# Gated delta rule in 64-chunks: a full inverse per chunk, multiplied into values and keys ahead of the chain over the chunks

## The chip, the core and the metric

The kernel runs on one core of a Trainium2 chip. A core has a matrix engine (TensorE, PE in the profile; PEld is its weight load), a vector engine (DVE), a scalar engine (ACT), a small general engine (POOL) and a queue processor that mostly issues DMA transfers (SP). Each runs its own list of instructions in order and waits on semaphores for the others. The metric is the device time of one execution in microseconds (us), the median over runs; lower is better.

## What is computed

The program is a chain of network blocks. Only the first one is touched: a hybrid block that sums a gated delta rule (8 heads of 64, both directions over 256 positions, chunks of 64) and a dilated-window attention. After it come a feed-forward layer, two mixers and a mixture of experts. The part of the reference that the change reorders:

```python
def gated_delta_rule_chunked(q, k, v, g, beta):
    ...
    kb = k * beta[..., None]
    a_low = jnp.where(strict, jnp.einsum('nhcid,nhcjd->nhcij', kb, k) * decay, 0.0)
    tmat = lax.linalg.triangular_solve(eye + a_low, eye, lower=True, unit_diagonal=True)
    u = jnp.einsum('nhcij,nhcjv->nhciv', tmat, v * beta[..., None])
    w = jnp.einsum('nhcij,nhcjk->nhcik', tmat, kb * jnp.exp(g)[..., None])
    ...
    def step(state, inp):
        u_i, w_i, qk_i, qd_i, kd_i, gl_i = inp
        v_new = u_i - jnp.einsum('nhck,nhkv->nhcv', w_i, state)
        o_i = jnp.einsum('nhck,nhkv->nhcv', qd_i, state) + jnp.einsum('nhij,nhjv->nhiv', qk_i, v_new)
        state = state * jnp.exp(gl_i)[..., None, None] + jnp.einsum('nhck,nhcv->nhkv', kd_i, v_new)
        return state, o_i
```

## The kernel before

Every large product is a gemm in three passes (lines 403, 404, 405: high part by high part, low by high, high by low), whose weights come by DMA in halves of 512 KB (`wr`) and are split by ACT and DVE (line 376) into `wh` and `wl`. These gemms use PSUM tiles `g`. The delta rule uses PSUM tiles `m` (three of them), the attention tiles `a` (two).

`delta()` (line 627) runs in the phase `mix1` beside gemms and attention. For each 128-row half t of the sequence and each direction d it makes `AQ[t, d]`: per head the triangular factor and the masked q-k product of two chunks of 64. The 32x32 diagonal blocks of the factor go through DRAM to one row per block, are inverted on DVE by a loop of 31 steps (lines 737 and 738), stored (line 739), and loaded back (line 747; for d = 1 turned on DVE, line 750) as `DT`. Beside that `kd` (k by decay) and `bv` (v by beta) are made on POOL (lines 762, 763), and k and q with their decays on DVE (line 766), turned by transposes on PE (line 770) and copied by ACT (line 771) into `kqd[t, d]`.

`delta_chain()` (line 782) then walks four chunks per direction, the two directions in turn. A step s has: p1 = (k with decay) times the state (line 797) and its subtraction on DVE (798), the solve with two inverted 32-blocks, that is a product (802) and copy on ACT (803), a product with the off-diagonal block (807) and subtraction on DVE (809), a product (813) and copy on ACT (814); then the new contribution to the state `pS` (820), the output `po` of q times state (824) and of the masked product (827), the decay of the state and the sum on DVE (837, 838; in step 0 a copy, 834), and the copy or sum of the output (841, 843). All of these are fp32 matrix products on tiles of 32x32, 64x64 or 128x64 of the PE array; one of them shows as two PE instructions in the trace.

Nothing in the block waits for the chain before `delta_out()`, which comes after the attention. The order in which each engine gets its instructions isn't written out: a scheduler with its own cost estimates merges delta rule, attention and gemms.

Of the kernel before, what the change touches and what calls it, by code (L numbers as in the profile page):

```python
# [17 lines left out]
AF = mybir.ActivationFunctionType  # L18
OP = mybir.AluOpType
# [30 lines left out]
P2 = (2, 1)  # L50
P3 = (2, 4)
P4 = (0, 1)
MIX1 = {"m": 3, "a": 2}, dict(s4=7, s2=13, s1=2, at3=5, ap=6, aq=4, on=2, dT=4)
FFN = {"m": 4, "n": 1}, dict(s4=5, s2=15, xr=4, xh=5, xl=5)
MIX2 = {"m": 3, "h": 2}, dict(s4=5, hx=2, m4=2, m2=6, h2=5, ti=4, tc=4, y=3, tg=4, hs=2, mix=2, od=2, s1=7)
MOE = {"m": 4, "g2": 1}, dict(s4=5, s2=8, xr=14, xh=4, xl=4)
# [209 lines left out]
class Prog:  # L266
# [360 lines left out]
    def delta(self):  # L627
        nc, mm = self.nc, self.nc.tensor.matmul

        y, m, e, l = (self.t("ty", [128, 2, 16]) for _ in range(4))  # L630
# [10 lines left out]
        be = self.t("dbe", [128, 2, 16])  # L641
# [16 lines left out]
        dec = self.t("ddec", [128, 8, 4])  # L658
# [13 lines left out]
        AQ = {}  # L672
# [64 lines left out]
            nc.vector.tensor_tensor(pv, av(U, 32 * i + m, [[0, m], [1, n]]), av(Y, i, [[32, m], [0, n]]), OP.mult)  # L737
            nc.vector.tensor_tensor(yv, yv, pv, OP.subtract)
        nc.sync.dma_start(Yd, Y)
        DT = {}  # L740
        for t in range(2):
            for d in range(2):
                dt_ = self.t("dT", [128, 8, 32], bufs=4) if d == 0 else self.t("s1", [128, 8, 32])
                for r in range(4):
                    src = bass.AP(tensor=Yd.tensor, offset=Yd.offset + (d * 64 + t * 4 + r) * 1024,
                                  ap=[[32, 32], [8 * 1024, 8], [1, 32]])
                    nc.sync.dma_start(dt_[32 * r:32 * r + 32], src)
                if d == 1:
                    o = self.t("dT", [128, 8, 32], bufs=4)
                    nc.vector.transpose(o, dt_)  # L750
                    dt_ = o
                DT[t, d] = dt_

        kd, bv, kqd = {}, {}, {}
        for d in range(2):
            for t in range(2):
                kqd[t, d] = self.t("s4" if d else "x", [128, 4, 2, 128])
                bc = lambda s: s[:, :, None].to_broadcast([128, 8, 64])
                hv = lambda x: x.rearrange("p (h e) -> p h e", h=8)
                q, k, v = (hv(self.qkv[a, t]) for a in range(3))  # L760
                kd[t, d], bv[t, d] = (self.t("s2", [128, 8, 64]) for _ in range(2))
                nc.gpsimd.tensor_tensor(kd[t, d], k, bc(ek[:, d, t]), OP.mult)
                nc.gpsimd.tensor_tensor(bv[t, d], v, bc(be[:, t, 8 * d:8 * d + 8]), OP.mult)
                for j, (src, sc) in enumerate(((k, bE[:, d, t]), (q, eG[:, d, t]))):
                    tmp = self.t("s2", [128, 8, 64])
                    nc.vector.tensor_tensor(tmp, src, bc(sc), OP.mult)
                    tf = tmp.rearrange("p h e -> p (h e)")
                    pt = self.p("m", [128, 4, 128])
                    for b in range(4):
                        nc.tensor.transpose(pt[:, b], tf[:, b * 128:b * 128 + 128], self.ident)  # L770
                    nc.scalar.activation(kqd[t, d][:, :, j], pt, AF.Copy)

        St = []
        for d in range(2):
# [1 line left out]
            nc.gpsimd.memset(s_, 0.0)  # L776
            St.append(s_)
        self.od = [self.t("s2", [128, 512]) for _ in range(2)]
        chains = [self.delta_chain(d, AQ, DT, bv, kd, kqd, St[d], dec) for d in range(2)]
        for _ in zip(*chains):  # L780
            pass
    def delta_chain(self, d, AQ, DT, bv, kd, kqd, St, dec):

        nc, mm = self.nc, self.nc.tensor.matmul
        for s in range(4):
            c = s if d == 0 else 3 - s
            t, a = c // 2, c % 2
            p0 = 64 * a
            q0, q1 = (p0, p0 + 32) if d == 0 else (p0 + 32, p0)
            b1 = 1 if d == 0 else 0  # L790
            P, Q0, Q1 = slice(p0, p0 + 64), slice(q0, q0 + 32), slice(q1, q1 + 32)
            cs = slice(a * 64, a * 64 + 64)
            v = u = bv[t, d]
            if s:
                p1 = self.p("m", [128, 4, 128])
                for b in range(4):
                    mm(p1[P, b], kqd[t, d][:, b, 0, cs], St[:, b], start=True, stop=True)
                nc.vector.tensor_tensor(u[P], u[P], p1[P].rearrange("p b (q e) -> p (b q) e", q=2), OP.subtract)
            yield
            p2 = self.p("m", [128, 8, 64])  # L800
            for h in range(8):
                mm(p2[Q0, h], DT[t, d][Q0, h], u[Q0, h], start=True, stop=True, tile_position=(q0, q0))
            nc.scalar.activation(v[Q0], p2[Q0], AF.Copy)
            yield
            p3 = self.p("m", [128, 8, 64])
            for h in range(8):
                mm(p3[Q1, h], AQ[t, d][Q0, h, 0, 32 * b1:32 * b1 + 32], v[Q0, h], start=True, stop=True,
                   tile_position=(q0, q1))
            nc.vector.tensor_tensor(u[Q1], u[Q1], p3[Q1], OP.subtract)
            yield  # L810
            p4 = self.p("m", [128, 8, 64])
            for h in range(8):
                mm(p4[Q1, h], DT[t, d][Q1, h], u[Q1, h], start=True, stop=True, tile_position=(q1, q1))
            nc.scalar.activation(v[Q1], p4[Q1], AF.Copy)
            yield
            if s < 3:
                pS = self.p("m", [128, 4, 64])
                for h in range(8):
                    L = slice(64 * (h % 2), 64 * (h % 2) + 64)
                    mm(pS[L, h // 2], kd[t, d][P, h], v[P, h], start=True, stop=True)  # L820
            po = self.p("m", [128, 4, 128])
            for b in range(4):
                if s:
                    mm(po[P, b], kqd[t, d][:, b, 1, cs], St[:, b], start=True, stop=False)
                for q in range(2):
                    h = 2 * b + q
                    mm(po[P, b, 64 * q:64 * q + 64], AQ[t, d][P, h, 1], v[P, h], start=(s == 0),
                       stop=(s == 0 or q == 1))
            if s < 3:
                for par in range(2):  # L830
                    L = slice(64 * par, 64 * par + 64)
                    sv = St[L, :, par]
                    if s == 0:
                        nc.vector.tensor_copy(sv, pS[L])
                    else:
                        dc = dec[L, (a * 2 + t) * 2 + d]
                        nc.vector.tensor_tensor(sv, sv, dc[:, :, None].to_broadcast([64, 4, 64]), OP.mult)
                        nc.vector.tensor_tensor(sv, sv, pS[L], OP.add)
            of = po[P].rearrange("p b n -> p (b n)")
            if s < 2:  # L840
                nc.scalar.activation(self.od[t][P], of, AF.Copy)
            else:
                nc.vector.tensor_tensor(self.od[t][P], self.od[t][P], of, OP.add)
            yield
# [1001 lines left out]
```

## Time and profile before

| | before |
|---|---|
| median of 3 runs (lowest to highest) | 2248.69 us (2246.05 to 2254.61) |
| profiled execution: its time | 2250.07 us |
| profiled execution: span | 2248.1 us |
| PE busy | 2185.7 us, 97% of the span |
| DVE busy | 1807.0 us, 80% |
| ACT busy | 1386.9 us, 62% |
| POOL busy | 38.7 us, 2% |

The delta rule's work lies between about 65 and 266 us of the span. An "idle before" is the time an engine stood still ahead of a group, with the engine and line that ended it. PEclk is the granted clock of PE as a share of 2.4 GHz: 1.00 is 2.4 GHz, 0.50 is 1.2 GHz, and a value between is a stretch with both. In the timeline the second number is the time from a group's start to its modelled end; matmuls overlap, so what a group takes of the engine is read from its start to the next group's start.

### The profile page before, as it was taken

Reading aid. Unit: us, or ns where it says so; the run is one execution under the profiler, and the core shown is the slowest. Engines: PE = TensorE matmul, PEld = TensorE weight load, DVE = VectorE, ACT = ScalarE, POOL = GpSimd, SP = SyncE. Lnnn points to the kernel's source line nnn. Section 1 sums busy time; section 2 is a strip of 40 time slices with the busy share of each in tenths; the row PEclk is TensorE's granted clock in tenths of the full one; section 3 lists DMA queues with packets and bytes.
Section 4 is the critical chain, followed back from the end, with each engine's and each line's share of the span. In section 5 each row is a group of like instructions: output and inputs, shape, how many; then the busy total and the mean of one; then the engine's idle time right before and its main releaser. Section 6 shows DMA issues by size and latency. Waiting matters only on the chain. (4 is left out here: it accounts for less than half of the span.)

```text
span 2248.1 us, 33817 instructions
## 1 busy us (share of the span) xinstructions
PE 2185.7 (97%) x12426; PEld 1862.6 (83%) x12426; DVE 1807.0 (80%) x2618; ACT 1386.9 (62%) x1854; POOL 38.7 (2%) x72
## 2 busy tenths in 40 slices
PE   7999999999999999999899999999999999999998
PEld 7787898999798878899787888788888888888886
DVE  6894367899868876878778876789899998989897
ACT  4553355554456565544258555588778888877885
POOL 0120000000000000000000000000000000000000
PEclk9999799999999999999999999999999999999999
DMA  6442254889364446888853445899999999999993
GB/s 200 123 145 73 66 154 147 327 293 317 117 206 144 131 145 206 302 289 301 292 187 118 147 150 174 309 346 357 341 369 348 346 363 337 357 343 367 349 352 137
DMA packets 164149, 549.41 MB, mean 244 GB/s; under 512 B 26632, under 2 KB 29320, under 8 KB 163976
## 3 DMA queue, kind: packets, MB, share of 16 engines
q1 hardware_dynamic: 163976, 547.18, 69.6%
q8 instruction: 99, 1.62, 0.3%
q14 instruction: 74, 0.61, 0.1%
HBM read 544.95 MB, written 2.11 MB: 243 GB/s over the span
## 5 line engine op out<-in xcount | busy, mean ns | idle before, releaser
L376 ACT ACTIVATE wh<-wr 128x1024 fp32r<-128x1024 f32 (+1 forms) x343 | 351.6, 1028 | 307.8 <-PE g L405 156.5
L376 DVE TENSOR_TENSOR wl<-wr,wh 128x1024 fp32r<-128x1024 f32 (+1 forms) x343 | 406.1, 1189 | 142.5 <-ACT wh L376 138.6
L376 DVE TENSOR_TENSOR xl<-xr,xh 128x1024 fp32r<-128x1024 f32 x282 | 338.1, 1221 | 26.2 <-ACT xh L376 18.2
L376 ACT ACTIVATE xh<-xr 128x1024 fp32r<-128x1024 f32 x282 | 295.8, 1061 | 73.7 <-PE g L405 29.4
L403 PE MATMUL g<-wh,xTH 128*128 128x512 f32 (+2 forms) x744 | 283.0, 382 | 5.4 <-ACT xTH L471 4.8
L404 PE MATMUL g<-wl,xTH 128*128 128x512 f32 (+2 forms) x744 | 281.2, 378 | 2.4 <-DVE wl L376 2.4
L405 PE MATMUL g<-wh,xTL 128*128 128x512 f32 (+2 forms) x744 | 281.9, 379 | 0.3 <-DVE xTL L472 0.3
L376 DVE TENSOR_TENSOR wl<-xr,wh 128x1024 fp32r<-128x1024 f32 x194 | 232.9, 1221 | 20.6 <-ACT wh L376 15.5
L376 ACT ACTIVATE wh<-xr 128x1024 fp32r<-128x1024 f32 x194 | 203.8, 1061 | 53.5 <-PE g L405 25.0
L403 PEld LDWEIGHTS g<-wh,xTH 128*128 128x128 f32 x744 | 143.1, 193 | 26.3 <-ACT xTH L471 5.6
L404 PEld LDWEIGHTS g<-wl,xTH 128*128 128x128 f32 x744 | 143.2, 192 | 24.0 <-DVE wl L376 3.9
L405 PEld LDWEIGHTS g<-wh,xTL 128*128 128x128 f32 x744 | 143.0, 192 | 22.1 <-issue 2.4
L403 PE MATMUL g<-xh,s 128*128 128x512 f32 x400 | 158.2, 396 | 0.0
L405 PE MATMUL g<-xh,s 128*128 128x512 f32 x400 | 156.4, 391 | 0.0
L404 PE MATMUL g<-xl,s 128*128 128x512 f32 x400 | 156.4, 391 | 0.0
L403 PE MATMUL g<-xTH,wh 128*128 128x256 f32 x528 | 151.3, 287 | 0.5 <-ACT wh L376 0.5
L404 PE MATMUL g<-xTL,wh 128*128 128x256 f32 x528 | 151.0, 286 | 0.1
L405 PE MATMUL g<-xTH,wl 128*128 128x256 f32 x528 | 150.4, 285 | 0.1
L376 ACT ACTIVATE xh<-wr 128x1024 fp32r<-128x1024 f32 x113 | 118.0, 1059 | 48.3 <-PE m L405 12.8
L376 DVE TENSOR_TENSOR xl<-wr,xh 128x1024 fp32r<-128x1024 f32 x113 | 135.8, 1220 | 11.9 <-ACT xh L376 10.1
L1130 DVE SCALAR_TENSOR_TENSOR macc<-rawm,cond,macc 128x1024 f32<-128x1024 f32 x84 | 107.6, 1281 | 34.4 <-DMA rawm<-in_wm_dram 33.8
L403 PE MATMUL g<-wh,s 128*128 128x512 f32 x320 | 126.8, 396 | 0.4 <-ACT s L471 0.4
(536 smaller groups left out, 4870.7 us busy)
## 6 DMA issues: line engine op xcount, KB each, us to landing
xr<-in_we_dram SPq DMA_DIRECT2D x412, 512.0 KB, 6.4
wr<-in_wb_dram SPq DMA_DIRECT2D x210, 512.0 KB, 4.8
wr<-in_we_dram SPq DMA_DIRECT2D x116, 512.0 KB, 6.1
rawm<-in_wm_dram SPq DMA_DIRECT2D x96, 512.0 KB, 5.6
wr<-in_wa_dram SPq DMA_DIRECT2D x82, 512.0 KB, 4.7
wr<-in_wt_dram SPq DMA_DIRECT2D x48, 384.0 KB, 3.1
xr<-in_wa_dram SPq DMA_DIRECT2D x32, 512.0 KB, 6.4
xr<-in_wb_dram SPq DMA_DIRECT2D x32, 512.0 KB, 8.4
```

The source lines that it names most:

```text
L376: self.behind((nc.scalar.activation(h, r, AF.Copy), nc.vector.tensor_tensor(l, r, h.bitcast(F), OP.subtract)))
L403: mm(ps, lh, rh, start=first, stop=False)
L404: mm(ps, lh, rl, start=False, stop=False)
L405: mm(ps, ll, rh, start=False, stop=last)
L1130: i = nc.vector.scalar_tensor_tensor(acc, raw, ck, acc, OP.mult, OP.add)
```

## The change

A new function `inverses()` builds, for each t and d, the whole (transposed) inverse of the 64-blocks in a tile `TT[t, d]`: the inverted 32-blocks are copied by ACT (new line 804) onto the diagonal of a zeroed tile, and the off-diagonal block is two 32x32 products, py (new line 816) and px (822), with a sign change on DVE between them (819) and a copy by ACT behind (824). From it come, outside of the chain, W (766, copied by ACT in 767 into `kqd[t, d][:, :, 0]`) and U (772, copied in 773). Only q is still transposed on PE (755). The product of v with beta moves from POOL to DVE (758). A step of the chain has left: W times state (837) with its subtraction on DVE (838), q times state into `po` (843; now all four ahead, in the same accumulation group), the decay of the state (848), `pS` (853) and its addition (860), and the masked product (864). `s4` gets an eighth buffer.

```diff
--- before.py
+++ after.py
@@ -50,7 +50,7 @@
 P2 = (2, 1)
 P3 = (2, 4)
 P4 = (0, 1)
-MIX1 = {"m": 3, "a": 2}, dict(s4=7, s2=13, s1=2, at3=5, ap=6, aq=4, on=2, dT=4)
+MIX1 = {"m": 3, "a": 2}, dict(s4=8, s2=13, s1=2, at3=5, ap=6, aq=4, on=2, dT=4)
 FFN = {"m": 4, "n": 1}, dict(s4=5, s2=15, xr=4, xh=5, xl=5)
 MIX2 = {"m": 3, "h": 2}, dict(s4=5, hx=2, m4=2, m2=6, h2=5, ti=4, tc=4, y=3, tg=4, hs=2, mix=2, od=2, s1=7)
 MOE = {"m": 4, "g2": 1}, dict(s4=5, s2=8, xr=14, xh=4, xl=4)
@@ -737,38 +737,40 @@
             nc.vector.tensor_tensor(pv, av(U, 32 * i + m, [[0, m], [1, n]]), av(Y, i, [[32, m], [0, n]]), OP.mult)
             nc.vector.tensor_tensor(yv, yv, pv, OP.subtract)
         nc.sync.dma_start(Yd, Y)
-        DT = {}
-        for t in range(2):
+        TT = self.inverses(Yd, AQ)
+
+        kd, U, kqd = {}, {}, {}
+        for t in range(2):
+            bc = lambda s: s[:, :, None].to_broadcast([128, 8, 64])
+            hv = lambda x: x.rearrange("p (h e) -> p h e", h=8)
+            q, k, v = (hv(self.qkv[a, t]) for a in range(3))
             for d in range(2):
...
                 kqd[t, d] = self.t("s4" if d else "x", [128, 4, 2, 128])
...
+                tq, tk = self.t("s2", [128, 8, 64]), self.t("s2", [128, 8, 64])
+                kd[t, d], U[t, d] = (self.t("s2", [128, 8, 64]) for _ in range(2))
+                nc.vector.tensor_tensor(tq, q, bc(eG[:, d, t]), OP.mult)
+                tf = tq.rearrange("p h e -> p (h e)")
+                pt = self.p("m", [128, 4, 128])
+                for b in range(4):
+                    nc.tensor.transpose(pt[:, b], tf[:, b * 128:b * 128 + 128], self.ident)
+                nc.scalar.activation(kqd[t, d][:, :, 1], pt, AF.Copy)
+
+                nc.vector.tensor_tensor(U[t, d], v, bc(be[:, t, 8 * d:8 * d + 8]), OP.mult)
+                nc.vector.tensor_tensor(tk, k, bc(bE[:, d, t]), OP.mult)
                 nc.gpsimd.tensor_tensor(kd[t, d], k, bc(ek[:, d, t]), OP.mult)
...
+                for a in range(2):
+                    P = slice(64 * a, 64 * a + 64)
+                    pw = self.p("m", [128, 4, 64])
+                    for h in range(8):
+                        L = slice(64 * (h % 2), 64 * (h % 2) + 64)
+                        mm(pw[L, h // 2], tk[P, h], TT[t, d][P, h], start=True, stop=True)
+                    nc.scalar.activation(kqd[t, d][:, :, 0, P], pw, AF.Copy)
+                pu = self.p("m", [128, 8, 64])
+                for a in range(2):
+                    P = slice(64 * a, 64 * a + 64)
+                    for h in range(8):
+                        mm(pu[P, h], TT[t, d][P, h], U[t, d][P, h], start=True, stop=True)
+                nc.scalar.activation(U[t, d], pu, AF.Copy)
 
         St = []
         for d in range(2):
@@ -776,66 +778,91 @@
             nc.gpsimd.memset(s_, 0.0)
             St.append(s_)
         self.od = [self.t("s2", [128, 512]) for _ in range(2)]
-        chains = [self.delta_chain(d, AQ, DT, bv, kd, kqd, St[d], dec) for d in range(2)]
+        chains = [self.delta_chain(d, AQ, U, kd, kqd, St[d], dec) for d in range(2)]
         for _ in zip(*chains):
             pass
-    def delta_chain(self, d, AQ, DT, bv, kd, kqd, St, dec):
+    def inverses(self, Yd, AQ):
+
+        nc, mm = self.nc, self.nc.tensor.matmul
+        TT, TP = {}, {}
+        for t in range(2):
+            TP[t] = self.t("s4", [128, 2, 8, 64])
+            nc.gpsimd.memset(TP[t], 0.0)
+        for t in range(2):
+            for d in range(2):
+                T = TT[t, d] = TP[t][:, d]
+
+                raw, turned = (self.t("dT", [128, 8, 32], bufs=4) for _ in range(2))
+                for r in range(4):
+                    src = bass.AP(tensor=Yd.tensor, offset=Yd.offset + (d * 64 + t * 4 + r) * 1024,
+                                  ap=[[32, 32], [8 * 1024, 8], [1, 32]])
+                    nc.sync.dma_start(raw[32 * r:32 * r + 32], src)
+                nc.vector.transpose(turned, raw)
+                across, plain = (raw, turned) if d == 0 else (turned, raw)
+                for r in range(4):
+                    R4 = slice(32 * r, 32 * r + 32)
+                    nc.scalar.activation(T[R4, :, 32 * (r % 2):32 * (r % 2) + 32], across[R4], AF.Copy)
+
+                py, px = self.p("m", [128, 8, 32]), self.p("m", [128, 8, 32])
+                y = self.t("s1", [128, 8, 32])
+                b1 = 1 - d
+                blocks = []
+                for a in range(2):
+                    p0 = 64 * a
+                    q0, q1 = (p0, p0 + 32) if d == 0 else (p0 + 32, p0)
+                    blocks.append((q0, q1, slice(q0, q0 + 32), slice(q1, q1 + 32)))
+                for q0, q1, Q0, Q1 in blocks:
+                    for h in range(8):
+                        mm(py[Q1, h], AQ[t, d][Q0, h, 0, 32 * b1:32 * b1 + 32], plain[Q0, h], start=True, stop=True,
+                           tile_position=(q0, q1))
+                for q0, q1, Q0, Q1 in blocks:
+                    nc.vector.tensor_scalar(y[Q1], py[Q1], -1.0, None, OP.mult)
+                for q0, q1, Q0, Q1 in blocks:
+                    for h in range(8):
+                        mm(px[Q0, h], y[Q1, h], across[Q1, h], start=True, stop=True, tile_position=(q1, q0))
+                for q0, q1, Q0, Q1 in blocks:
+                    nc.scalar.activation(T[Q0, :, 32 * b1:32 * b1 + 32], px[Q0], AF.Copy)
+        return TT
+    def delta_chain(self, d, AQ, U, kd, kqd, St, dec):
 
         nc, mm = self.nc, self.nc.tensor.matmul
         for s in range(4):
             c = s if d == 0 else 3 - s
             t, a = c // 2, c % 2
...
+            P = slice(64 * a, 64 * a + 64)
+            v = U[t, d]
             if s:
                 p1 = self.p("m", [128, 4, 128])
                 for b in range(4):
-                    mm(p1[P, b], kqd[t, d][:, b, 0, cs], St[:, b], start=True, stop=True)
-                nc.vector.tensor_tensor(u[P], u[P], p1[P].rearrange("p b (q e) -> p (b q) e", q=2), OP.subtract)
+                    mm(p1[P, b], kqd[t, d][:, b, 0, P], St[:, b], start=True, stop=True)
+                nc.vector.tensor_tensor(v[P], v[P], p1[P].rearrange("p b (q e) -> p (b q) e", q=2), OP.subtract)
             yield
...
+            po = self.p("m", [128, 4, 128])
+            if s:
+                for b in range(4):
+                    mm(po[P, b], kqd[t, d][:, b, 1, P], St[:, b], start=(b == 0), stop=False)
+                if s < 3:
+                    for par in range(2):
+                        L = slice(64 * par, 64 * par + 64)
+                        sv, dc = St[L, :, par], dec[L, (a * 2 + t) * 2 + d]
+                        nc.vector.tensor_tensor(sv, sv, dc[:, :, None].to_broadcast([64, 4, 64]), OP.mult)
             if s < 3:
                 pS = self.p("m", [128, 4, 64])
                 for h in range(8):
                     L = slice(64 * (h % 2), 64 * (h % 2) + 64)
                     mm(pS[L, h // 2], kd[t, d][P, h], v[P, h], start=True, stop=True)
...
                 for par in range(2):
                     L = slice(64 * par, 64 * par + 64)
                     sv = St[L, :, par]
                     if s == 0:
                         nc.vector.tensor_copy(sv, pS[L])
                     else:
-                        dc = dec[L, (a * 2 + t) * 2 + d]
-                        nc.vector.tensor_tensor(sv, sv, dc[:, :, None].to_broadcast([64, 4, 64]), OP.mult)
                         nc.vector.tensor_tensor(sv, sv, pS[L], OP.add)
+            for b in range(4):
+                for q in range(2):
+                    h = 2 * b + q
+                    mm(po[P, b, 64 * q:64 * q + 64], AQ[t, d][P, h, 1], v[P, h], start=(s == 0),
+                       stop=(s == 0 or h == 7))
             of = po[P].rearrange("p b n -> p (b n)")
             if s < 2:
                 nc.scalar.activation(self.od[t][P], of, AF.Copy)
```

The order of PE in the middle of the delta rule. Before, in step 1 and 2 of the chain (`m` are the delta rule's PSUM tiles, `g` the gemms', `wh` and `wl` split weights, `x` and `s4` tiles at the right of 797 are `kqd`):

```order
L797 MATMUL m_242_1328<-s2_216_1094,x_195_1031 64x128 x4
L405 MATMUL g_498_2530<-wh_492_2519,xTL_4_69 128x512
L403 MATMUL g_498_2530<-wh_492_2519,xTH_3_68 128x512
L404 MATMUL g_498_2530<-wl_493_2520,xTH_3_68 128x512
L797 MATMUL m_243_1334<-s2_217_1096,s4_202_1052 64x128 x4
L405 MATMUL g_498_2530<-wh_492_2519,xTL_4_69 128x512
L403 MATMUL g_497_2529<-wh_495_2525,xTH_3_68 128x512
L802 MATMUL m_244_1340<-s2_197_1033,dT_185_998 32x64 x8
L802 MATMUL m_245_1350<-s2_204_1054,dT_184_996 32x64 x8
L404 MATMUL g_497_2529<-wl_496_2526,xTH_3_68 128x512
L405 MATMUL g_497_2529<-wh_495_2525,xTL_4_69 128x512
```

After, at the place where W and U are made, between the last gemms beside the inverses and the chain (`s4_182` and `s4_183` are the inverses, `s2_...` at the right of 766 the scaled k):

```order
L755 MATMUL m_218_1249<-ident_5_72,s2_214_1244 128x128 x4
L766 MATMUL m_219_1258<-s4_182_986,s2_215_1245 64x64 x8
L766 MATMUL m_220_1268<-s4_182_986,s2_215_1245 64x64 x8
L772 MATMUL m_221_1278<-s2_217_1247,s4_182_986 64x64 x16
L755 MATMUL m_227_1302<-ident_5_72,s2_223_1297 128x128 x4
L766 MATMUL m_228_1311<-s4_183_988,s2_224_1298 64x64 x8
L766 MATMUL m_229_1321<-s4_183_988,s2_224_1298 64x64 x8
L772 MATMUL m_230_1331<-s2_226_1300,s4_183_988 64x64 x16
L755 MATMUL m_236_1355<-ident_5_72,s2_232_1350 128x128 x4
L766 MATMUL m_237_1364<-s4_183_988,s2_233_1351 64x64 x8
L766 MATMUL m_238_1374<-s4_183_988,s2_233_1351 64x64 x8
L772 MATMUL m_239_1384<-s2_235_1353,s4_183_988 64x64 x16
```

Before, gemm instructions stand between the small products of a step; after, 12 groups of transposes, W and U follow each other with none between.

DVE at the first attention block, before (`aq` are the attention's q and k that PE turns next, `dbE` and `deG` decays):

```order
L719 STREAM_TRANSPOSE s2_177_909<-s2_178_910 128x512
L766 TENSOR_TENSOR s2_191_1015<-s2_75_471,dbE_139_757 128x512
L766 TENSOR_TENSOR s2_193_1023<-s2_51_313,deG_137_755 128x512
L556 TENSOR_TENSOR aq_282_1634<-aq_282_1634,ty_321_1808 128x384
L766 TENSOR_TENSOR s2_198_1036<-s2_76_473,dbE_139_757 128x512
L766 TENSOR_TENSOR s2_200_1044<-s2_52_315,deG_137_755 128x512
L556 TENSOR_TENSOR aq_283_1636<-aq_283_1636,ty_321_1808 128x384
L556 TENSOR_TENSOR aq_298_1712<-aq_298_1712,ty_321_1808 128x384
L556 TENSOR_TENSOR aq_299_1714<-aq_299_1714,ty_321_1808 128x384
L766 TENSOR_TENSOR s2_205_1057<-s2_75_471,dbE_139_757 128x512
L376 TENSOR_TENSOR wl_366_1961<-wr_364_1958,wh_365_1960 128x1024
```

After:

```order
L719 STREAM_TRANSPOSE s2_177_909<-s2_178_910 128x512
L751 TENSOR_TENSOR s2_205_1191<-s2_51_313,deG_137_755 128x512
L758 TENSOR_TENSOR s2_208_1194<-s2_107_663,dbe_134_744 128x512
L759 TENSOR_TENSOR s2_206_1192<-s2_75_471,dbE_139_757 128x512
L751 TENSOR_TENSOR s2_214_1244<-s2_51_313,deG_137_755 128x512
L758 TENSOR_TENSOR s2_217_1247<-s2_107_663,dbe_134_744 128x512
L759 TENSOR_TENSOR s2_215_1245<-s2_75_471,dbE_139_757 128x512
L556 TENSOR_TENSOR aq_282_1702<-aq_282_1702,ty_321_1876 128x384
L751 TENSOR_TENSOR s2_223_1297<-s2_52_315,deG_137_755 128x512
L556 TENSOR_TENSOR aq_283_1704<-aq_283_1704,ty_321_1876 128x384
L556 TENSOR_TENSOR aq_298_1780<-aq_298_1780,ty_321_1876 128x384
L556 TENSOR_TENSOR aq_299_1782<-aq_299_1782,ty_321_1876 128x384
```

Before, two scalings stand ahead of the first product for `aq` (line 556 in both); after, six stand ahead of it, and on PE the transposes of line 770 that came in between are gone.

## Rows read from the trace of the kernel before

**Rows 1.** Section 1 of the page: busy us (share of the span) and instructions.

```profile
PE 2185.7 (97%) x12426; PEld 1862.6 (83%) x12426; DVE 1807.0 (80%) x2618; ACT 1386.9 (62%) x1854; POOL 38.7 (2%) x72
```

**Rows 2.** Windows of 20 us: length, busy us of each engine, PEclk, DMA share, GB/s.

```profile
100.00:120.00 20.00, 15.79 (x95) 12.46 (x90) 19.45 (x21) 8.23 (x14) 13.31 (x12) 1.00 0.37 100
...
200.00:220.00 20.00, 20.00 (x217) 14.75 (x216) 7.74 (x14) 4.72 (x8) 0.00 (x0) 1.00 0.15 47
220.00:240.00 20.00, 19.79 (x208) 14.78 (x205) 7.58 (x14) 4.91 (x9) 0.00 (x0) 1.00 0.07 21
240.00:260.00 20.00, 20.00 (x145) 15.75 (x145) 4.85 (x7) 3.92 (x6) 0.00 (x0) 0.62 0.21 60
260.00:280.00 20.00, 20.00 (x100) 17.77 (x100) 7.67 (x11) 9.26 (x16) 0.55 (x2) 0.78 0.38 114
```

**Rows 3.** Windows of 2 us at the fall and rise of the clock.

```profile
242.00:244.00 2.00, 2.00 (x27) 1.67 (x25) 0.74 (x1) 0.59 (x1) 0.00 (x0) 1.00 0.16 14
244.00:246.00 2.00, 2.00 (x23) 1.73 (x21) 0.00 (x0) 0.59 (x1) 0.00 (x0) 0.74 0.53 183
...
268.00:270.00 2.00, 2.00 (x10) 2.00 (x10) 0.96 (x1) 1.22 (x3) 0.00 (x0) 0.78 0.00 0
```

**Rows 4.** Lines of PE from 60 to 300 us: count, busy us, mean ns, idle before.

```profile
L827 PE MATMUL m<-s,s 64*64 64x64 f32 x128 | 14.8, 251 | 0.0
...
L802 PE MATMUL m<-s,dT 32*32 32x64 f32 x128 | 8.2, 216 | 0.0
...
L770 PE MATMUL m<-ident,s 128*128 128x128 f32 x32 | 5.2, 284 | 4.0 <-DVE s L766 3.9
...
L820 PE MATMUL m<-s,s 64*64 64x64 f32 x96 | 4.1, 224 | 0.0
```

**Rows 5.** Timeline of PE at full clock: start, us to the modelled end, group.

```profile
105.61 0.39 PE L403 MATMUL g<-wh,xTH 128*128 128x512 f32 x1
105.84 0.39 PE L404 MATMUL g<-wl,xTH 128*128 128x512 f32 x1
...
195.68 1.14 PE L827 MATMUL m<-s,s 64*64 64x64 f32 x16
196.75 0.51 PE L403 MATMUL g<-wh,xTH 128*128 128x512 f32 x1
...
227.35 1.07 PE L813 MATMUL m<-s,dT 32*32 32x64 f32 x16
228.35 0.50 PE L404 MATMUL g<-wl,xTH 128*128 128x512 f32 x1
228.78 0.68 PE L820 MATMUL m<-s,s 64*64 64x64 f32 x16
229.40 0.43 PE L824 MATMUL m<-s,x 128*64 128x128 f32 x2
...
230.13 0.43 PE L824 MATMUL m<-s,x 128*64 128x128 f32 x2
...
237.62 1.09 PE L797 MATMUL m<-s,x 128*64 128x128 f32 x8
238.64 0.45 PE L404 MATMUL g<-wl,xTH 128*128 128x384 f32 x1
```

**Rows 6.** Timeline of PE at half clock.

```profile
244.91 1.89 PE L807 MATMUL m<-s,s 32*32 32x64 f32 x16
...
254.86 0.69 PE L824 MATMUL m<-s,x 128*64 128x128 f32 x2
...
256.09 0.69 PE L824 MATMUL m<-s,x 128*64 128x128 f32 x2
```

**Rows 7.** Lines of ACT from 60 to 300 us.

```profile
L803 ACT ACTIVATE s<-m 32x512 f32<-32x512 f32 x8 | 4.7, 589 | 9.9 <-PE m L802 9.6
```

**Rows 8.** Lines of DVE from 60 to 300 us.

```profile
L809 DVE TENSOR_TENSOR s<-s,m 32x512 f32<-32x512 f32 x8 | 5.5, 684 | 14.3 <-PE m L807 14.2
...
L766 DVE TENSOR_TENSOR s<-s,deG 128x512 f32<-128x512 f32 x4 | 4.4, 1104 | 0.0
```

More of the change, by code (lines that the diff above doesn't have):

```diff
@@ L739, in delta @@
         nc.sync.dma_start(Yd, Y)
-        DT = {}
+        TT = self.inverses(Yd, AQ)
+        kd, U, kqd = {}, {}, {}
         for t in range(2):
+            bc = lambda s: s[:, :, None].to_broadcast([128, 8, 64])
+            hv = lambda x: x.rearrange("p (h e) -> p h e", h=8)
+            q, k, v = (hv(self.qkv[a, t]) for a in range(3))
             for d in range(2):
[L743 to L752, printed above, removed]
@@ L754, in delta @@
-        kd, bv, kqd = {}, {}, {}
-        for d in range(2):
-            for t in range(2):
-                kqd[t, d] = self.t("s4" if d else "x", [128, 4, 2, 128])
[L758 to L761, printed above, removed]
-                nc.gpsimd.tensor_tensor(kd[t, d], k, bc(ek[:, d, t]), OP.mult)
[L763 to L771, printed above, removed]
+                kqd[t, d] = self.t("s4" if d else "x", [128, 4, 2, 128])
@@ L787, in delta_chain @@
             t, a = c // 2, c % 2
[L788 to L793, printed above, removed]
+            P = slice(64 * a, 64 * a + 64)
+            v = U[t, d]
             if s:
@@ L796, in delta_chain @@
                 for b in range(4):
-                    mm(p1[P, b], kqd[t, d][:, b, 0, cs], St[:, b], start=True, stop=True)
-                nc.vector.tensor_tensor(u[P], u[P], p1[P].rearrange("p b (q e) -> p (b q) e", q=2), OP.subtract)
+                    mm(p1[P, b], kqd[t, d][:, b, 0, P], St[:, b], start=True, stop=True)
+                nc.vector.tensor_tensor(v[P], v[P], p1[P].rearrange("p b (q e) -> p (b q) e", q=2), OP.subtract)
             yield
[L800 to L815, printed above, removed]
+            po = self.p("m", [128, 4, 128])
[7 more added lines that the diff above has]
+                        nc.vector.tensor_tensor(sv, sv, dc[:, :, None].to_broadcast([64, 4, 64]), OP.mult)
             if s < 3:
@@ L820, in delta_chain @@
                     mm(pS[L, h // 2], kd[t, d][P, h], v[P, h], start=True, stop=True)
[L821 to L829, printed above, removed]
                 for par in range(2):
```

## The prediction, made blind

> **What bounds the kernel now.** First the engines' shares on the page: PE is busy 97% of the span, DVE 80%, ACT 62% [rows 1]. So time is won or lost only where PE gets less or more to do, waits, or runs at another clock. Then windows of 20 us over the stretch in which the delta rule runs. PE is full there, 20.00 of 20.00 us between 200 and 280 but for 0.21 us [rows 2]; it does not wait for the chain, since between two small products the scheduler gives it gemms. Two things stand out. From 100 to 120 us PE is idle for 4.21 us [rows 2], nearly all of it before the transposes of line 770, which wait for the scalings on DVE [rows 4]. And the granted clock is 0.62 from 240 to 260 and 0.78 from 260 to 280 [rows 2]: in the 2 us windows it falls within 244 to 246, on the way to half rate (0.74), and comes back within 268 to 270 (0.78) [rows 3], so half rate from about 245.0 to 269.1, 24 us. PE was busy for all of the window before the fall [rows 3]; what it had done there were mostly the small fp32 products of the chain.
>
> So the change is counted in PE time: the instructions it takes and gives, two waits, and the clock.
>
> **The change part by part.** Prices are from one start to the next at full clock. 16 instructions on one 32x32 tile: 227.35 to 228.35, 1.00 us; line 820, whose products alternate between two column tiles, 0.62 (228.78 to 229.40); line 827, 64x64 on one tile, 1.07 (195.68 to 196.75); 8 instructions of line 797, 1.02 (237.62 to 238.64); a pair of 824 with its 827, 0.73 (229.40 to 230.13) [rows 5].
>
> Small products before. Lines 802, 807 and 813 have 8 groups of 16 each (x128 in the trace [rows 4]): 24 x 1.00 = 24.0. Line 820: 6 groups (x96 [rows 4]), 3.7. Line 797, 6 x 1.02 = 6.1. The output with state: 6 outputs of 4 pairs, 24 x 0.73 = 17.5; the two of step 0, 2 x 1.07 = 2.1. Transposes of 770: 5.2 [rows 4]. Sum 58.6 us.
>
> After. py and px: for 4 (t, d) and 2 products, 16 matmuls of two instructions each, 16 groups of 16. They are not in the trace. They have a 32x32 tile as line 802, but move 32 columns, not 64: above, the price of line 802, 1.00; below, half of it is too little as soon as something other than columns counts, and the cheapest row with 16 instructions is line 820 with 0.62. Bounds 9.9 to 16.0; I take 0.85, nearer to the row with the same tile, so 13.6. W: 8 groups like line 820, 5.0. U: 8 like line 827, 8.6. Transposes of q alone: half of 5.2, 2.6. In the chain: W times state, 6.1 as line 797; q times state, four together, like line 797 too, 6.1; pS 3.7; the masked product, 8 x 1.07 = 8.6. Sum 54.3, bounds 50.6 and 56.7. The gain is 4.3 us (1.9 to 8.0). In words: 24 groups of the solve go, 16 + 8 + 8 come, and what pays is mostly that pairs of 824 and 827 are sorted (17.5 becomes 6.1 + 6 x 1.07 = 12.5).
>
> A pair costs 0.73 where a quarter of line 797's eight and a quarter of line 827's sixteen would be 0.26 + 0.27 = 0.52 [rows 5]: each pair, with two changes of tile size, loses 0.21. The Trainium skill ("TensorEngine Tiling (Array Packing)", section "Key Properties") says that changing the tiling mode drains TensorE, which those 0.21 agree with. By that rule py, px and W, set between gemms in some 20 places with two changes each, would cost about 4 us more, and the 4.3 us would be nearly nothing; the rows of line 802 in the sum were taken between gemms too, so I leave it out.
>
> DVE and POOL at 105 to 120 us. The transposes of line 770 leave this place, and their 4.0 us of waiting [rows 4] with them. But the products for `aq` (line 556), for which PE turns next, now stand behind six scalings and not two. A scaling takes 0.68 alone (line 809 has as many columns and 0.684), and 1.10 on average beside POOL [rows 8]: four more are 2.7 to 4.4 us later for `aq`. PE has 15 gemm instructions ahead of that wait in the new order, 3.5 us at 0.23 each (105.61 to 105.84 [rows 5]), where before it had its first transposes. Bounds of the gain: 0 (the new wait is as long) and 4.2; I take 1.5, since the four extra cost about what the old waits did. Moving v by beta from POOL to DVE is in this count.
>
> New waits. py waits for a copy, then DVE's negation (0.68 at most by line 809 [rows 8]), then px, then ACT's copy (0.589 by line 803 [rows 7]); gemms stand between in the order for most. In the stretch of W and U there is none: per t and d 0.65 of transposes, 1.24 of W and 2.14 of U on PE against 4 copies of ACT, 2.4 us, through three PSUM tiles. So ACT keeps up on the average, but a group can wait for the copy of the third tile before. 16 such copies and 8 of the inverse: nothing if all are hidden, 24 x 0.589 = 14.1 if none is. I take 4, nearer to hidden, because PE's own work in a group is longer than the copy. The chain itself is shorter: a step of one direction has one subtraction on DVE instead of four stops, and while it waits, PE has the other direction.
>
> The clock. At half rate 16 instructions of line 807 take 1.89, the modelled time (1.07 for as many at full rate), a pair 1.23 (254.86 to 256.09) and not 0.73 [rows 5, 6]: 41 to 43% of the half-rate time is lost, and half of it in the gemms at its end. 24 us x 0.45 = 11 us that before pays. After pays X instead.
>
> Sum: -4.3 - 1.5 + 4 - 11 + X = -12.8 + X. The clock has fallen once in this stretch in a mix of gemms and small products, and the new order is denser in small ones in its second half (12 groups, 16 us, with no gemm, then the chain), but has gemms between the inverses before and a run of gemms sooner behind. That the clock stays up all the way is not safe; I take X = 3, a short fall. So -9.8 against the profiled execution, 2250.07, which stood 1.4 us above the median: 2248.69 - 9.8 = 2239 us.
>
> **Rivals.**
>
> A. The same loss of clock again, X = 11: -1.8, 2247 us. For it: the new stretch has as many small products (54.3 against 58.6 us), and the fall in the trace came without any pause of PE. Against it: the stretch is cut in another way.
>
> B, slower. The clock falls before W and U and stays at half rate until the chain has ended, because nothing there but small products feeds PE; before, the gemms after 266 us are what stands where it rises. Place: from the last inverse to the end of the chain, W 5.0, U 8.6, q 2.0, chain 24.5, and some gemms, together about 41 us of full-rate work. Price: at 1.23 / 0.73 = 1.7 times, 29 us. So -12.8 + 29 = +16, 2265 us. It decides from 13 / 0.7 = 18 us of such work at half rate on, less than half of the stretch. For it: gemms between the products are what this order takes away. Against: from 200 to 240 us small products had most of PE, and the clock was 1.00 [rows 2].
>
> C. Each eviction is waited for: +14 and not +4, with X = 3: 2249 us. For it: the order has no gemm between W and U. Against: ACT is half idle there.
>
> D. The clock does not fall at all, X = 0, and the wait at 105 us goes whole: -4.3 - 4.2 + 3 - 11 = -16.5, 2232 us, where evictions cost 3. The Trainium skill ("TensorE: Matmul & The Clock Gate", section "Why this matters for your kernels") states that throughput drops come from idle gaps between matmul bursts. The trace disagrees: PE was busy 2.00 of 2.00 us ahead of the fall [rows 3]. By that rule a denser stretch would never fall, and D would be the forecast.
>
> **How the numbers follow.** Chances: forecast (X from 0 to 6 and the two bounded waits, 2231 to 2246) 0.36, D 0.20, A 0.14, C 0.06, B 0.24. The range 2228 to 2266 holds all but the lowest part of D and the upper half of B, less than 2 in 10; the likeliest case alone has 2231 to 2246. What a measurement of this kernel can tell from no change is about 0.5%, 11 us. Faster than 2237.5: D, and a little under half of the forecast, 0.20 + 0.17 = 0.37. Slower than 2260: B, 0.24. Between: the rest of the forecast, A and C, 0.39.
>
> **What would show it.** Right: PEclk 1.00 in nearly all windows from 200 to 285 us, the first transposes of the attention's second block sooner by some 10 us, line 770's successor with no idle ahead of it, groups of py and px at 0.6 to 1.0 us. B would show as PEclk 0.50 beside lines 766, 772, 843 and 864, C as idle of PE ahead of 766 and 772 ended by ACT. The forecast is wrong if the stretch before the second attention block changes by less than 3 us, or if the difference arises after it, where PE's order is the same.

## The result and the profile after

The changed kernel takes 2226.06 us (2220.87 to 2227.58, 4 runs) where the kernel before, run beside it, takes 2247.68: ratio 0.9894, 95% interval 0.9867 to 0.9921. By the ratio the change is faster by 1.1%; the medians are 21.6 us apart. 2239 us was forecast, some 9 us less than before, with 2228 as the lower end. So the sign was right and the size more than double what was forecast. One execution of the kernel before, beside the later runs, took 12180 us and is left out of every ratio and spread here.

The first page section of after, and windows of 20 us over the delta rule, against [rows 1, 2] (a window has its length, busy us of PE, PEld, DVE, ACT and POOL, PEclk, DMA share and GB/s):

```profile
PE 2163.1 (97%) x12538; PEld 1851.8 (83%) x12538; DVE 1804.6 (81%) x2624; ACT 1390.7 (63%) x1870; POOL 35.9 (2%) x70
```

```profile
100.00:120.00 20.00, 17.67 (x92) 14.57 (x91) 19.46 (x38) 9.16 (x15) 10.03 (x13) 1.00 0.44 120
...
180.00:200.00 20.00, 19.76 (x210) 14.74 (x208) 7.11 (x11) 10.12 (x20) 0.00 (x0) 0.93 0.34 89
200.00:220.00 20.00, 20.00 (x390) 18.03 (x388) 7.25 (x12) 11.78 (x26) 4.46 (x7) 1.00 0.09 22
220.00:240.00 20.00, 19.98 (x249) 17.33 (x247) 13.00 (x27) 2.87 (x4) 0.00 (x0) 1.00 0.23 69
240.00:260.00 20.00, 20.00 (x127) 19.78 (x125) 12.54 (x25) 11.67 (x18) 1.60 (x3) 1.00 0.57 171
```

Three things are to be seen. PE lost 22.6 us of busy time (2185.7 to 2163.1), the span 24.7 (2248.1 to 2223.4). The clock is at 1.00 all through W, U and the chain (200 to 240), where before it was 0.62 and 0.78 from 240 to 280. And PE is full there, in the stretch without gemms too: no copy makes it wait.

Where the time went is read at one instruction, the first transpose for the third of the attention's four blocks (the prediction and the expectations call it the second). From it on PE's order is the same in both kernels, but for a dozen gemm instructions far behind. Timeline of PE, before and then after:

```profile
286.83 0.82 PE L876 MATMUL a<-ident,aq 128*128 128x128 f32 x6
```

```profile
261.98 0.82 PE L903 MATMUL a<-ident,aq 128*128 128x128 f32 x6
```

24.85 us sooner. Behind it the difference swings between 18 and 27 us, since both kernels have further spells of half rate at other places, and at PE's last instruction it is 25.0. So on balance all of the gain lies ahead of this point. Below, "the mark" is this start.

To split it, the starts of PE's instructions from 104 us to the mark were subtracted from the next starts and added by line. Small fp32 products of the delta rule: 62.6 us before, of which 16.6 lie in the half-rate stretch, and 43.2 after. At half rate 0.42 of a small product's time is lost (the prediction's 41 to 43%), so 7.0 of the 16.6 are the clock. A gemm of 384 columns takes 0.32 us there from start to start and 0.17 at full clock, so of the 7.4 us of gemms in that stretch 3.4 are. The clock cost 10.4 us before. After, half rate lasts from 179.5 to 182.9; an execution of the same kernel without it had the mark 1.6 us sooner (the last run below). That gives 8.8 us from the clock, 55.6 - 43.2 = 12.4 us from small products at full clock, and 3.6 us that are left over, from waits and from changes of tile that this sum books with the gemms. In the same stretch the tile size changes 119 times from one PE instruction to the next before and 68 times after, although the small products have 736 instructions before and 848 after. Lines that PE waited for, in before and then in after (us in total, times, longest):

```profile
PE a L876 <- DVE aq L556: 1.3, 2, 0.7
```

```profile
PE a L903 <- DVE aq L556: 2.2, 4, 1.1
PE a L925 <- ACT at L904: 0.7, 1, 0.7
```

The waits of after answer to this 1.3 us and the 4.0 us before line 770 [rows 4].

The small products, timeline of PE in the changed kernel (start, us to the modelled end, group):

```profile
184.73 0.69 PE L816 MATMUL m<-dT,s 32*32 32x32 f32 x16
185.35 0.50 PE L404 MATMUL g<-wl,xTH 128*128 128x512 f32 x1
...
192.97 1.07 PE L816 MATMUL m<-dT,s 32*32 32x32 f32 x32 [0.24 <-DVE dT L800]
193.96 0.50 PE L404 MATMUL g<-wl,xTH 128*128 128x512 f32 x1
...
207.65 1.79 PE L772 MATMUL m<-s,s 64*64 64x64 f32 x31
209.37 0.66 PE L755 MATMUL m<-ident,s 128*128 128x128 f32 x4
```

16 instructions of py between gemms take 0.62 us, 32 take 0.99: about 0.4 for each 16, and 0.2 once for the change from a gemm and back. U, 31 instructions in a run, takes 1.72, or 0.89 for 16, where line 827 between gemms took 1.07 [rows 5].

### The profile page after: what moved, and what is told of

Same layout as the page of the kernel before. It is cut to its first block, busy times and chain, and to the rows that moved or that the text cites. A ratio compares the mean times of both kernels' runs of the same rounds, so it can differ in the third digit from the quotient of the medians.

```text
span 2223.4 us, 34058 instructions
## 1 busy us (share of the span) xinstructions
PE 2163.1 (97%) x12538; PEld 1851.8 (83%) x12538; DVE 1804.6 (81%) x2624; ACT 1390.7 (63%) x1870; POOL 35.9 (2%) x70
## 5 line engine op out<-in xcount | busy, mean ns | idle before, releaser
L376 DVE TENSOR_TENSOR wl<-xr,wh 128x1024 fp32r<-128x1024 f32 x194 | 232.8, 1220 | 21.6 <-ACT wh L376 16.0
L404 PEld LDWEIGHTS g<-wl,xTH 128*128 128x128 f32 x744 | 141.9, 191 | 24.7 <-DVE wl L376 4.9
```

The lines of the kernel that those rows point to most:

```text
L376: self.behind((nc.scalar.activation(h, r, AF.Copy), nc.vector.tensor_tensor(l, r, h.bitcast(F), OP.subtract)))
L404: mm(ps, lh, rl, start=False, stop=False)
```

## The experiments

Theory: two shares, the half-rate stretch (brought about, it says, by the solve's 32x32 products in the chain) and cheaper small products, because fewer changes of tile stand between them. "Mark" is as above; half rate is by the trace's clock records between 100 us and the mark. Both come from one profiled execution of each kernel. Each ratio is to executions of the kernel before that were run beside it, with medians of 2247.60 to 2254.62. "Sooner" and "later" compare marks, with that of the first trace of before or after if nothing else is said; after's two traces differ by 1.6 us. Half rate costs about 0.45 of its length (1.6 of 3.4 there).

| kernel | median us | ratio to before, interval | mark | half rate, from to |
|---|---|---|---|---|
| before | 2247.68 | | 286.83 | 245.0 to 268.9 |
| after | 2226.06 | 0.9894 (0.9867 to 0.9921) | 261.98 | 179.5 to 182.9 |
| outputs sorted, in before | 2243.97 | 0.9965 (0.9927 to 1.0002) | 281.42 | 221.3 to 245.2 |
| pairs back, in after | 2230.63 | 0.9938 (0.9912 to 0.9964) | 268.34 | none |
| inverse in the chain | 2228.51 | 0.9898 (0.9862 to 0.9934) | 267.91 | 117.2 to 124.0, 199.1 to 202.5 |
| no solve, in before | 2212.39 | 0.9832 (0.9797 to 0.9867) | 249.88 | none |
| py, px twice | 2239.86 | 0.9961 (0.9943 to 0.9980) | 276.71 | 181.7 to 202.2 |
| W, U twice | 2233.26 | 0.9926 (0.9899 to 0.9953) | 272.74 | 115.3 to 122.1 |
| scalings later | 2225.14 | 0.9886 (0.9854 to 0.9919) | 264.90 | 178.1 to 191.7 |
| and tiles in turn | 2220.15 | 0.9864 (0.9835 to 0.9892) | 260.49 | 168.8 to 172.2, 179.0 to 192.7 |
| 64-row products added | 2267.42 | 1.0066 (1.0039 to 1.0093) | 306.41 | 115.5 to 122.4, 183.8 to 207.7, 214.5 to 258.9 |
| no py, px | 2214.11 | 0.9813 (0.9773 to 0.9853) | 254.08 | 114.3 to 124.5 |
| tiles in turn alone | 2215.83 | 0.9835 (0.9804 to 0.9867) | 254.69 | none |
| after again | 2223.57 | 0.9868 (0.9838 to 0.9899) | 260.41 | none |

**Outputs sorted.** In the kernel before:

```diff
+            if s:
+                for b in range(4):
+                    mm(po[P, b], kqd[t, d][:, b, 1, cs], St[:, b], start=(b == 0), stop=False)
             for b in range(4):
-                if s:
-                    mm(po[P, b], kqd[t, d][:, b, 1, cs], St[:, b], start=True, stop=False)
                 for q in range(2):
```

> The kernel before, with only the output products sorted: the four products of q with the state first, then the eight masked ones, instead of pairs. The place to read is the start of PE's first transposes for the second attention block (286.8 us before, 262.0 after). Theory 'two shares' (about 11 us of the 24.9 are the half-rate stretch, which the 32x32 products of the solve inside the chain bring about, and about 13 us are small products in longer runs with fewer changes of tile): only the pairs' changes go, 3 to 5 us, the half-rate stretch stays, 282 to 284. Rival 'sorting is the gain': 270 or less, and no half-rate stretch.

Measured: 5.4 us sooner. The half-rate stretch is as long as before, 24 us, only earlier. So in this execution the sorting is its own small term, and does not keep the clock up. For the whole program the interval reaches 1.0002, and the executions differ: three of ten took 2230.2 to 2230.6 us at a mean granted clock of 0.992 or 0.993, where the kernel before has 0.979 to 0.989. They have no trace; that the half-rate stretch is missing in them is likely and not shown.

**Pairs back.** The reverse edit in the changed kernel, with the decay behind the outputs.

> The changed kernel with the outputs in pairs again and the decay of the state behind them, as before. Theory 'two shares': 4 to 6 us later, 266 to 268, full clock in the chain. Rival 'sorting is the gain': 272 or later, with half rate in the chain.

Measured: 6.4 us later than the first trace of after, and 7.9 later than the second, which has no half rate either and is the fairer measure; 4 to 6 were expected. The small products take 49.9 us and not 43.2, and the tile size changes 113 times and not 68. The decay stands elsewhere too, so not all of it need be the pairs. Here are two pairs in it:

```profile
224.33 0.43 PE L848 MATMUL m<-s,s 128*64 128x128 f32 x2
224.69 0.44 PE L851 MATMUL m<-s,s 64*64 64x64 f32 x4
225.06 0.43 PE L848 MATMUL m<-s,s 128*64 128x128 f32 x2
```

0.73 us each, as before. The tile changes at every second to fourth instruction.

**Inverse in the chain.** W and U go, each step gets

```diff
+            pu = self.p("m", [128, 8, 64])
+            for h in range(8):
+                mm(pu[P, h], TT[t, d][P, h], v[P, h], start=True, stop=True)
+            nc.scalar.activation(v[P], pu[P], AF.Copy)
```

> The changed kernel with the full inverses, but not applied outside of the chain: k and q are turned as before, and each step multiplies the inverse into (beta v - k times state), one 64x64 product of 8 with a copy by ACT. So W and U are gone, and each step has one stop more. Theory 'two shares': PE has about as much small work (W 3.6 goes, transposes of k 2.4 come), no 32x32 products in the chain, full clock there: 261 to 265. Rival 'it is the place outside of the chain': the stops bring gemms between the products again, 8 us or more later, 270 to 275, with half rate possible.

Measured: 5.9 us later than after, between the two ranges. Half rate stands in two short spells outside of the chain; it cost some 10.2 x 0.45 = 4.6 against 1.6, so 3 us of the 5.9 are the clock. The chain itself runs at 1.00 (window 220 to 240). The full inverse has most of the gain; its place outside of the chain has some 3 us.

**No solve.** In before, p2, p3 and p4 are gone.

> The kernel before with the solve left out of every step (the two products with inverted 32-blocks and the one with the off-diagonal block, their copies and subtraction): u goes on as v, so the output is not the reference's. Theory 'two shares': 24 groups of 16 instructions at 1.0 us go, and with them the 24 us of half rate (about 11): 250 to 254. Rival 'any small products make the clock fall': the half-rate stretch stays, 260 to 265.

Measured: 36.95 us sooner, without half rate. 249.88 is just under the 250 to 254 expected of 24 groups and the clock.

**py and px twice.** Both loops `for _ in range(2):`.

> The changed kernel with every product of py and px issued twice (the second writes the same). Theory 'two shares' with its law of runs (in the changed kernel's trace 16 instructions between gemms take 0.62 us and 32 take 1.02, so 0.22 for the two changes and 0.40 for each 16): 16 x 0.40 = 6.4 us more if the clock stays, first transposes of the second attention block at 268.4 and not 262.0; and if the 32x32 products are what brings the clock down, longer half rate at 176 to 205 us, 2 to 8 us more. Rival (each 16 instructions cost 0.62 to 1.00 wherever they stand): 10 to 16 us more, 272 to 278. Rival on the clock (the share of gemms decides, not the kind of product): half rate no longer than the 3.4 us.

Measured: 14.7 us later, at the upper end of what was expected and inside the rival's 272 to 278, so that the total does not decide. The timeline does: the law of runs holds, 64 instructions take 1.84 us (0.22 + 4 x 0.40 = 1.82), and the clock fell for 20.5 us, about 9.2 us of loss. All ten executions have a mean granted clock of 0.981 to 0.988, those of after 0.989 to 0.993. Timeline, then a window:

```profile
177.60 1.91 PE L817 MATMUL m<-dT,s 32*32 32x32 f32 x64
179.44 0.50 PE L403 MATMUL g<-wh,xTH 128*128 128x512 f32 x1
```

```profile
180.00:200.00 20.00, 20.00 (x217) 15.52 (x216) 4.59 (x8) 6.88 (x14) 0.00 (x0) 0.54 0.12 28
```

**W and U twice.** `for h in (*range(8), *range(8))` in W, `for a in (0, 1, 0, 1)` in U.

> The changed kernel with every product of W and U issued twice. There are no gemms between them, so this makes the stretch without gemm 30 and not 20 us long. Theory 'two shares': 10.2 us more (W 3.6 and U 6.7 again), 272, and full clock, since these are 64x64 products. Rival on the clock (a long stretch without gemms is enough): half rate from there to the end of the chain, 20 us more or above.

Measured: 10.8 us later, and 1.00 in the doubled stretch, with no gemm from 203 to 229 us:

```profile
200.00:220.00 20.00, 20.00 (x457) 18.33 (x454) 5.44 (x7) 8.82 (x20) 4.24 (x7) 1.00 0.14 40
220.00:240.00 20.00, 20.00 (x366) 18.43 (x363) 8.27 (x18) 4.92 (x9) 0.00 (x0) 1.00 0.09 29
```

So a long stretch without gemms does not bring the clock down by itself; all five executions have mean clocks of 0.991 to 0.993. The 6.8 us of half rate at 115 us in this trace stand where PE's order is that of after, which was at full clock there in both traces. Such a spell differs from execution to execution.

**64-row products added.** Ahead of py, and likewise ahead of px:

```diff
+                for a in range(2):
+                    for h in range(8):
+                        P = slice(64 * a, 64 * a + 64)
+                        mm(py[P, h], AQ[t, d][P, h, 1], plain[P, h], start=True, stop=True)
```

> The changed kernel with as many products added as the run with py and px twice had (256, of 32 columns each, at the same places), but on 64x64 tiles: ahead of py and of px, into the same PSUM tiles, overwritten or never read. Theory '32x32 products bring the clock down': half rate no longer than 3 to 7 us about there, against 20.5 us with the 32x32 products twice; the first transposes of the second attention block at 269 to 272. Rival (the amount of small products beside the gemms decides): half rate 15 us or more, 275 to 282.

Measured: 44 us later, outside of both ranges, and the only kernel slower than before. All ten executions have a low mean clock, 0.973 to 0.978. The clock fell at 183.8 behind the first such products, rose at 207.7 in a run of gemms, fell again at 214.5, and then stayed at half rate through W, U and the first part of the chain:

```profile
180.00:200.00 20.00, 20.00 (x235) 17.84 (x234) 3.31 (x8) 4.72 (x11) 0.00 (x0) 0.60 0.13 29
200.00:220.00 20.00, 20.00 (x204) 16.30 (x204) 4.32 (x7) 5.07 (x10) 0.00 (x0) 0.67 0.25 66
220.00:240.00 20.00, 20.00 (x246) 18.23 (x245) 4.44 (x6) 5.61 (x13) 2.24 (x3) 0.50 0.01 2
240.00:260.00 20.00, 20.00 (x228) 18.10 (x228) 2.38 (x5) 5.71 (x11) 1.90 (x5) 0.53 0.01 2
```

The theory's 3 to 7 us are refuted: 64x64 products beside the gemms lengthen half rate too, to 68 us behind 180 us, where as many 32x32 ones gave 20.5. That no 32x32 products are needed is not shown, since those of py and px are still there. Here line 820 is py, and 817 and 827 are the added ones:

```profile
180.22 1.84 PE L817 MATMUL m<-dT,s 64*64 64x32 f32 x32
181.99 1.09 PE L820 MATMUL m<-dT,s 32*32 32x32 f32 x32
183.01 2.61 PE L827 MATMUL m<-dT,s 64*64 64x32 f32 x32
```

In the traces of the table, nine falls between 160 us and the mark have no gap of PE right before them. Each came during 32x32 products or at most 1.3 us behind them. The run also shows the slower rival of the prediction at work in part: W, U and the first part of the chain do not fall by themselves, but did not rise either when they were entered at half rate. The clock came back at 258.9, behind three gemms, and the rest of the chain, to about 280, ran at full rate.

**No py, px.** Left out with the negation and the copies.

> The changed kernel without the off-diagonal blocks: py, px, the negation and the copies are left out, the inverse stays with its diagonal 32-blocks, so the output is not the reference's. Theory: no half rate between 160 and 260 us, and py and px's 9.1 us gone, with 1.5 us of clock: 251.5 for the first transposes of the second attention block. Rival: half rate at the same place after the attention's products.

Measured: 254.08, with no half rate from 160 on, but 10 us of it at 114 to 124, which is worth 10.2 x 0.45 = 4.6. Without that it is 249.5, near the 251.5 expected.

**Scalings later**, and **tiles in turn**. The scalings got an order behind the last subtraction of line 738; in the second also:

```diff
-                for a in range(2):
-                    P = slice(64 * a, 64 * a + 64)
-                    for h in range(8):
+                for h in range(8):
+                    for a in range(2):
+                        P = slice(64 * a, 64 * a + 64)
                         mm(pu[P, h], TT[t, d][P, h], U[t, d][P, h], start=True, stop=True)
```

> The changed kernel with the 12 scalings on DVE (q, k and v by their factors) behind the last step of the inversion loop. Theory: the waits of the first attention block's transposes and scores (2.2 and 0.7 us idle) go, nothing else: 259 for the first transposes of the second attention block. Rival (a new wait in their place, of the W products for the scalings, or of gemms for the splitting on DVE behind them): 262 or later.

> As the run before, and the products of py, px and U take the two 64-halves in turn (head by head) instead of one half after the other, so that neighbours lie on different tiles of the array. W, whose neighbours lie on two column tiles, costs 0.024 us per instruction in the changed kernel's trace, U 0.054 on one tile. Theory: U falls from 6.7 to about 3.6 us and py and px from 9.1 to about 7: 259 less 5, 254. Rival (only column tiles of the same rows overlap): no change by it, 259.

Measured: the first is 2.9 us later at the mark, as the rival had it, and over the whole program 0.9 less than after. The waits at 105 us are gone (PE 20.00 of 20.00), but from 160 to 180 PE now idles 1.4 us for an instruction of the attention on DVE, and the clock is down for 13.6 us:

```profile
100.00:120.00 20.00, 20.00 (x121) 16.63 (x120) 15.58 (x37) 10.18 (x18) 9.40 (x13) 1.00 0.49 140
160.00:180.00 20.00, 18.60 (x162) 15.12 (x161) 15.89 (x30) 10.80 (x21) 9.70 (x12) 0.95 0.54 147
180.00:200.00 20.00, 20.00 (x168) 15.78 (x168) 6.29 (x16) 7.93 (x19) 0.00 (x0) 0.71 0.15 32
```

The second is 4.4 us before the first, not at the 254 expected. In it the turns pay, the scalings don't, so they were run apart.

**Tiles in turn alone**, beside **after again**.

> The changed kernel with py, px and U taking the two 64-halves in turn, and the scalings where the change has them. By the run with both, U costs 4.2 and not 6.7, py and px 6.8 and not 9.1: 5 us less than the changed kernel if the clock falls no longer, 257, and by the profile's whole 2221; if it falls for 13 us as in the runs with the scalings later, 261 and 2226, the same as the changed kernel.

> The changed kernel itself beside these: 2226, first transposes of the second attention block at 262, if the 3.4 us of half rate at 180 us are the rule; up to 5 us later if in other executions the clock falls for longer there.

Measured: 254.69 and 260.41 at the mark, both without half rate, and 2215.83 us (2212.29 to 2221.50, 6 runs) against 2223.57 (2221.28 to 2227.26). This version beats both kernels: 0.9835 of before, 0.35% less than the change alone, with ranges that just touch. U in it:

```profile
202.90 1.15 PE L772 MATMUL m<-s,s 64*64 64x64 f32 x32
203.99 0.66 PE L755 MATMUL m<-ident,s 128*128 128x128 f32 x4
```

32 instructions take 1.09 us, where 31 took 1.72 one tile after the other: neighbours on two tiles overlap in part.

## Why the prediction missed its size

1. **The sum of small products failed: its prices were too high.** "Sum 54.3, bounds 50.6 and 56.7": it was 43.2. The sum of before, 58.6, was 55.6 at full clock. So these products gave 12.4 us and not 4.3, which is 8.1 of the 15 us that the forecast lacked. Two steps were wrong.
   - The price of py and px. "Half of it is too little" led to 0.85 for 16 instructions; between gemms they took 0.62, the lower bound. Less the 0.22 of the change, 16 instructions with 32 columns take 0.40, and 16 with 64 columns (1.00 [rows 5], if the change costs the same there) 0.78. With half of the groups in runs of 32 beside that, 13.6 became 9.1, under the lower bound of 9.9.
   - The changes of tile. The other prices were a group's time between gemms and held a change; after, most groups stand in runs and share it. U was predicted at 8.6 and took 6.7; W 5.0 and 3.6; W times state 6.1 and 4.5. The run with 64 instructions settles it: 0.22 for the change, 0.40 for 16. The order of the changed kernel showed these runs, and the prediction read them only as a danger to the clock.
2. **The waits for copies, +4, were none.** In W and U PE is busy 20.00 of 20.00 us. Three PSUM tiles were enough.
3. **The wait at 105 us was right in size.** 1.5 us of gain were predicted; the waits named in the trace went from 4.0 and 1.3 (for `aq`) to 2.2 and 0.7, a gain of 2.4, of which PE's idle time from 100 to 120 us shows 1.9 (4.21 to 2.33). Of the 4.21, 0.66 stood before `aq` already, and not before line 770 as nearly all was read to.
4. **The clock was right in size.** The 11 us lost before were 10.4; X = 3 was 1.6, and nothing in the execution run again. That X came near is in part luck: no row gave it, and spells of this length come and go between executions. Of the cases D, 2232 us, came nearest, and it had the same sum of products. A and B did not come; B's mechanism exists in part, as the added products showed.
5. **Sorted outputs**, 5.0 predicted, were 5.4 in before, and 7.9 in after at the same clock with the decay's place in it.

With the terms as measured the sum is -8.8 - 12.4 - 2.4 = -23.6, of the 24.85.

The Trainium skill ("TensorEngine Tiling (Array Packing)", "Key Properties") has it that a change of the tiling mode drains TensorE, and the prediction weighed it as speaking against the change. The rows agree that a change costs something, about 0.2 us for a pair of them. That the new kernel would add changes was wrong, since it takes more of them away: 119 became 68. The Trainium skill ("TensorE: Matmul & The Clock Gate", "Why this matters for your kernels") ties drops to idle gaps. The traces agree only in part. With the inverse in the chain, half rate from 117.2 follows a gap:

```profile
114.32 1.18 PE L896 MATMUL a<-ident,aq 128*128 128x128 f32 x6 [1.46 <-DVE aq L556]
```

After had gaps of 1.07, 0.34 and 0.67 us at about the same place and stayed at full clock in both traces. The falls at 245 before and at 184 with the 64-row products follow no gap; PE was busy all the time there.

**Open.** What in a busy stretch brings the clock down is not settled. That 32x32 products alone count is refuted, and so is the mere lack of gemms; whether it comes without any 32x32 products beside is untested, since no run took py and px out and put 64x64 products in their place. Shown is only that half rate in the chain was in the traces of both kernels with the three-part solve in it, and in none without that solve, but for the one with 64-row products added. So how much the clock gave, 8.8 us, is measured, and why the new order keeps it up is not.

## To carry to other kernels

Price a small matrix product twice, alone between larger ones and in a run, and count the changes of tile in the new order: sorting equal shapes together, and setting neighbours on different tiles, was worth more here than the number of instructions. Look at the granted clock of each stretch before counting instructions: half rate, once there, lasted 3.4 to 44 us here, and everything that stood in it paid. A stall that is taken away can come back as another, as the scalings did; the mark at which both orders join again shows it.

## What was not expected of the hardware

A 64x64 product of 32 columns costs as much as one of 64: 32 instructions of the added ones took 1.77 us at full clock (180.22 to 181.99), 0.055 each, and those of U 0.055. On a 32x32 tile the columns count: 0.40 for 16 instructions with 32 of them and about 0.78 with 64. Executions of the kernel before spread from 2239 to 2264 us, with mean granted clocks from 0.989 in the quicker to 0.979 in the slower ones; those of the change from 2221 to 2228 with 0.989 to 0.993. The time goes with the clock; in which stretch it differs between them was not looked at.
